# Where a delayed norm, a weight preparation and an activation store stand in the queues: three moves in a one-layer hybrid kernel

## The chip, the cores and the metric

The kernel runs on one core of a Trainium2 chip, as one launch. The metric is the device time of the program in microseconds (us): the median of several runs. The engines are TensorE (PE, with its weight loads as PEld), VectorE (DVE), ScalarE (ACT), GpSimd (POOL) and SyncE (SP). SP, ACT and POOL can issue DMAs; each works through its instructions in order, so that an issue that has to wait holds up whatever stands behind it on that engine.

## The reference

One layer of a streaming encoder for two groups of rows that share the weights: one prompt of 2048 rows and 8 sample sequences of 16 rows, all 1024 wide.

```python
h   = rms_norm(x, norm_g[0])
z   = h @ w_in                        # q, k, v of attention and of the mLSTM, gates
att = rms_norm(chunk_band_attention(z), g_att)        # 8 heads x 64
ml  = head_norm(mlstm(z)) * g_mlstm * sigmoid(o)      # 4 heads x 128
x   = x + rms_norm(concat([att, ml]) @ w_out, norm_g[1])          # "x2" below
u   = rms_norm(x, norm_g[2]) @ w_up                               # 2 x 2816 columns
y   = causal_conv(u, w_conv, width=3) + b_conv
gate, up = split(y)
x   = x + rms_norm((gelu(gate) * up) @ w_down, norm_g[3])
```

The outputs are the new rows and the new caches of attention, mLSTM and convolution.

## The kernel before, in words

The rows are cut into 17 tiles of 128 (16 of the prompt, one of the samples). Matrices are multiplied in a split form: both operands are written as a rounded part and a rest (`hi`, `lo`; names ending in `h` and `l`), and each product is three matmuls, lines L104, L105 and L106 of one helper. The split of a weight takes a CAST on ACT (`wuh`, L1301) and a subtraction on DVE (`wul`, L1302).

*Order.* The instructions are not run in the order of the code. A scheduler simulates a timeline and puts the instructions of each engine into an order by it. Instructions wrapped in `tc.keep_in_program_order` keep the code's order among themselves. Stages are written as generators that yield where other work may come between.

*The project stage* (`project`, 1052 to 1352 us in the trace) goes over the tiles: it loads the mixed rows (`mr`, L991), norms them, turns them (PE transposes into `mT_pt`; ACT writes the rounded part `mt` by a CAST, L210, DVE the rest, L211), multiplies by `w_out` into `wo` in two halves, copies each half out on DVE (L1029), sums squares on ACT (L1031), scales on DVE (L1041), adds the input row on POOL (L1042), and stores the result as `x2d` (L1043). The input row of a later tile is loaded into `mx` on SP (L1018) and waits for the buffer that the store of x2 reads. Beside this, the first part of the FFN begins: rows of x2 come back (`x2r`, L1084), ACT squares them (L1100), and the first up weights are fetched (`wu`, L1318) and combined (`ws`, L1330).

*The down-weight differences* (`folds`) are a preparation that runs beside the project stage. The FFN uses one level of a scheme with seven products in place of eight, which needs differences of the blocks of `w_down`. For each of `NK` = 11 groups, four blocks of 128x512 are loaded from `in_w_down` (SP, L1178), four differences are formed in place (DVE, L1183), and four blocks are stored to `wtd` in HBM (POOL, L1186). `project` steps this generator 4 times a tile.

*The FFN* runs in three blocks of 6, 6 and 5 tiles, each with an up stage over 22 features and a down stage. In an up stage the products of a feature are followed by copies on ACT and by additions (`uu`), the convolution (`y`, L1513 and L1514) and the gate (`g`, L1672 and L1675) on DVE, while SP fetches later weights (`wu`, L1348), each as soon as its buffer is free.

*Delayed norms.* The last norm of blocks 0 and 1 is done in the next block's up stage. The down stage has stored its result as `f0d` and `f1d`, two halves of 512 columns for each tile. `later` makes one unit for each half tile: it fetches the half into `f` (L1436) and the half row of x2 into `x` (L1437), multiplies by the row's factor and the norm's gains on DVE (L1439), adds `x` on POOL (L1440) and stores the output from POOL (L1441). `delayed` steps the units, once for each feature from the fourth on; there are 12 units in block 1's up stage and 12 in block 2's.

*Buffers.* `spare` is a pool of 6 buffers of 128x512 for one thing after another: four for a group of `folds`, two for a unit of `later`.

Of the kernel before, what the change touches and what calls it, by code (L numbers as in the profile page):

```python
# [13 lines left out]
ALU = mybir.AluOpType  # L14
# [26 lines left out]
NK = NF // 2  # L41
# [8 lines left out]
def hymba_step(ctx: ExitStack, tc: tile.TileContext, I: dict, O: dict):  # L50
    nc = tc.nc
# [17 lines left out]
    def spare_tile(name):  # L69
        return spare.tile([P, 512], F32, tag="k", name=name)  # L70

    def dt_(shape, name):
        return dram.tile(shape, F32, tag=name, name=name)
# [15 lines left out]
    def rsqrt_mean(ssq, n, name, eps=EPS):  # L89
        ms = small.tile([P, 1], F32, tag="ms", name=name + "_ms")  # L90
        mean_square(ms, ssq, n, eps)
        rs = small.tile([P, 1], F32, tag="rs", name=name + "_rs")
        nc.gpsimd.tensor_tensor(rs, ms, nhalf[:, 0:1], op=ALU.pow)  # L93
        return rs
# [30 lines left out]
    wtd = [dt_([P, 2048], f"wtd{k}") for k in range(NK)]  # L125
    wsd = [dt_([P, 2048], f"wsd{f}") for f in range(NF)]
    lated = [dt_([P, 4, 384], f"lated{i}") for i in range(4)]
    x2d = [dt_([P, D], f"x2d{t}") for t in range(17)]

    def x_src(t):  # L130
        return I["x_sample"] if t == SAMPLE else I["x_prompt"][t * P:(t + 1) * P, :]
# [69 lines left out]
    def rows_to_T(hrow, chunk, j, name, bank):  # L201
        w = 4 if bank is not ps_big else KT
        for q in range(KT // w):
            pt = bank(f"{name}_pt{q}")
            for k in range(w):
                transpose(pt[:, k * P:(k + 1) * P], hrow[:, (w * q + k) * P:(w * q + k + 1) * P])
            ptv = pt.rearrange("p (k t) -> p k t", k=w)
            hv = chunk[:, 0, w * q:w * q + w, j * P:(j + 1) * P]
            lv = chunk[:, 1, w * q:w * q + w, j * P:(j + 1) * P]
            nc.scalar.copy(hv, ptv)  # L210
            nc.vector.tensor_tensor(lv, ptv, hv, op=ALU.subtract)  # L211
# [4 lines left out]
    def rows_tile(tag, shape, name, dtype=F32):  # L216
        if tag == "xr":
            return rows.tile(shape, dtype, tag="xr", name=name, bufs=2)
        return pa.tile(shape, dtype, tag=tag, name=name, bufs=1)
# [750 lines left out]
    def drain():  # L970
        while any([p_.step() for p_ in pipes]):
            pass

    def project(tiles):

        ss = [SimpleNamespace(t=t) for t in tiles]
        fold = folds(3, 2)

        def load(s):
            t = s.t  # L980
            if t == 8:
                drain()
                open_ffn()
            s.m = rows_tile("xr", [P, D], f"mr{t}")
            if t == SAMPLE:
                for b in range(DB):
                    own = bass.AP(atts[b].tensor, atts[b].offset, [[512, DS], [DS * 512 + DA, HA], [1, DA]])
                    nc.sync.dma_start(s.m[b * DS:(b + 1) * DS, 0:512].rearrange("p (h d) -> p h d", h=HA), own)
                nc.sync.dma_start(s.m[:, 512:D], mixs)
            else:  # L990
                nc.sync.dma_start(s.m, mixd[t // 4][:, t % 4, :])  # L991

        def norm(s):
            mt = wpool.tile([P, 2112], F32R, tag="wh", name=f"mt{s.t}", bufs=2)
            ssq = small.tile([P, 1], F32, tag="ssq", name=f"assq{s.t}")
            nc.scalar.activation(mt[:, :512], s.m[:, :512], AF.Square, accum_out=ssq)
            rs = rsqrt_mean(ssq, 512, f"att{s.t}")
            nc.vector.tensor_scalar(s.m[:, :512], s.m[:, :512], rs, None, op0=ALU.mult)
            s.mt = mt[:, :2 * D].rearrange("p (a k n) -> p a k n", a=2, k=KT)

        def turn_rows(s):
            ffn.mt = s.mt
            rows_to_T(s.m, s.mt, 0, f"mT{s.t}", ps_mm if s.t < 8 else ps_big)

        load(ss[0])
        norm(ss[0])
        yield 0.0, 0.3
        turn_rows(ss[0])
        load(ss[1])
        yield 0.9, 1.2  # L1010
        for n_, s in enumerate(ss):
            t = s.t
            nxt = ss[n_ + 1] if n_ + 1 < len(ss) else None
            if nxt:
                norm(nxt)
            mx = wpool.tile([P, 2112], F32, tag="wl", name=f"mx{t}", bufs=2)
            m, xr = mx[:, 0:D], mx[:, D:2 * D]
            nc.sync.dma_start(xr, x_src(t))  # L1018
            for hf in range(2):
                c = slice(hf * 512, hf * 512 + 512)  # L1020
                acc = ps_mm(f"wo{t}_{hf}")
                for k in range(KT):
                    mm3(acc, s.mt[:, 0, k, :], s.mt[:, 1, k, :], wo[k][0][:, c], wo[k][1][:, c],
                        start=(k == 0), stop=(k == KT - 1))
                    if k % 4 == 3:
                        next(fold, None)
                        yield 2.6, 0.5
                ssq = small.tile([P, 1], F32, tag="wssq", name=f"wssq{t}_{hf}")
                nc.vector.tensor_copy(m[:, c], acc)  # L1029
                idle = m[:, 512:D] if hf == 0 else s.mt[:, 0, 0:4, :].rearrange("p k n -> p (k n)")  # L1030
                nc.scalar.activation(idle, m[:, c], AF.Square, accum_out=ssq)  # L1031
                if hf == 0:
                    ssa = ssq
                    mean_square(ssa, ssq, D)
                    if nxt:
                        turn_rows(nxt)
                        if n_ + 2 < len(ss):
                            load(ss[n_ + 2])
                        yield 0.9, 1.2
            rs = rsqrt_mean(ssq, D, f"n1_{t}", ssa)  # L1040
            nc.vector.scalar_tensor_tensor(m, m, rs, g1[0], op0=ALU.mult, op1=ALU.mult)  # L1041
            nc.gpsimd.tensor_tensor(xr, m, xr, op=ALU.add)  # L1042
            nc.gpsimd.dma_start(x2d[t], xr)  # L1043
        for _ in fold:
            pass

# [7 lines left out]
    def open_ffn():  # L1054

        p1.close()
        ffn.p3 = ctx.enter_context(tc.tile_pool(name="p3", bufs=2, reuse_waits="tile"))
        ffn.halo = ffn.p3.tile([P, 44, 2], F32, tag="halo", name="halo", bufs=1)
        nc.vector.memset(ffn.halo, 0.0)
        ffn.g2 = ffn.p3.tile([P, D], F32, tag="g2", name="g2", bufs=1)  # L1060
        nc.sync.dma_start(ffn.g2, I["norm_g"][2:3, :].broadcast_to([P, D]))
        pipes[:] = [Pipe(h2_units(0, lead=6)), Pipe(iter([]))]
# [107 lines left out]
            nc.scalar.copy(hi, lo.bitcast(F32))  # L1170
            nc.vector.tensor_tensor(lo, lo.bitcast(F32), hi, op=ALU.subtract)

    def folds(before, after):

        for k in range(NK):
            t = [spare_tile(f"fold{k}_{x}") for x in range(4)]
            for x in range(4):
                tc.keep_in_program_order(nc.sync.dma_start(t[x], I["w_down"][k][:, x * 512:(x + 1) * 512]))  # L1178
            for _ in range(before):
                yield  # L1180
            a, b, c, d = t
            for o, x, y in ((a, b, a), (b, c, b), (c, c, a), (d, d, c)):
                tc.keep_in_program_order(nc.vector.tensor_tensor(o, x, y, op=ALU.subtract))  # L1183
            yield
            for x in range(4):
                tc.keep_in_program_order(nc.gpsimd.dma_start(wtd[k][:, x * 512:(x + 1) * 512], t[x]))  # L1186
            for _ in range(after):
                yield

    GROUPS = ["va0", "qk0", "qk1", "va1", "qk2", "qk3", "qb0", "vo0", "qb1", "vo1", "qb2", "vo2", "qb3", "vo3"]  # L1190
    SRC = {g: i for i, g in enumerate(["va0", "qk0", "qk1", "va1", "qk2", "qk3",
# [45 lines left out]
    for n_, (half, gi) in enumerate(seq):  # L1237
        wh, wl, _ = pend
# [193 lines left out]
    def later(t, rs):  # L1432

        def unit(half):
            v, x, c = spare_tile(f"f{half}{t}"), spare_tile(f"x{half}{t}"), half * 512
            tc.keep_in_program_order(nc.sync.dma_start(v, (f0d, f1d)[half][t]))  # L1436
            tc.keep_in_program_order(nc.sync.dma_start(x, x2d[t][:, c:c + 512]))  # L1437
            yield 0.0, 0.0
            nc.vector.scalar_tensor_tensor(v, v, rs, g3[:, c:c + 512], op0=ALU.mult, op1=ALU.mult)  # L1439
            nc.gpsimd.tensor_tensor(v, v, x, op=ALU.add)  # L1440
            nc.gpsimd.dma_start(out_rows(t)[:, c:c + 512], v)  # L1441
            yield 0.0, 1.0

        return [unit(half) for half in range(2)]

    def delayed(units):

        for u, after in zip(units, units[1:] + [iter([])]):
            if u is units[0]:
                next(u)  # L1450
                yield
            next(after, None)
            next(u)
            yield

    ph.close()
    p4 = ffn.p4 = ctx.enter_context(tc.tile_pool(name="p4", bufs=1, side="right", reuse_waits="tile"))
# [3 lines left out]
    g3 = norm_row(3)  # L1461
# [14 lines left out]
    for b, tiles in enumerate(FBLOCKS):  # L1476
# [282 lines left out]
        for dh in range(2):  # L1759
# [57 lines left out]
            for j in order:  # L1817
# [5 lines left out]
                else:  # L1823
# [4 lines left out]
                    rs = p3.tile([P, 1], F32, tag=f"drs{j}", name=f"drs{tiles[j]}", bufs=2)  # L1828
# [101 lines left out]
```

## Time and profile before

| what | value |
|---|---|
| median of 3 runs | 2822.27 us (2820.95 to 2822.5) |
| the profiled execution's own time | 2824.88 us |
| its span | 2823.1 us |
| its granted PE clock, mean | 0.988 |
| PE busy | 2709.4 us, 96% of the span |
| DVE, ACT, POOL busy | 1877.5, 1516.3 and 646.3 us |
| project stage | 1052 to 1352 us |
| delayed norms in block 1's and block 2's up stage | about 1895 to 2095 and 2384 to 2558 us |

A row of waits reads: engine and line of the instruction that waited, what released it, us in total, times, the longest. A row of the timeline reads: start and duration in us, engine, line, operation, output and inputs, and in square brackets how long the engine had been idle before it and for what. A row of windows gives for each engine how long it was busy in the window, the clock that PE was granted (1.00 is full) and the share of time in which the DMA engines moved data. "SPq" is SP's queue.

### The profile page before, as it was taken

How to read it: one execution, taken by the hardware profiler on the slowest of the kernel's cores; microseconds unless marked ns; L12 is line 12 of the kernel's file. 1: busy time of each engine (PE TensorE's matmuls, PEld its weight loads, DVE VectorE, ACT ScalarE, POOL GpSimd, SP SyncE). 2: the span in 40 equal slices, each digit the busy share in tenths (PEclk: the TensorE clock that was granted, in tenths of full speed). 3: DMA queues.
4: the chain of work that ended last, by engine and by line, in shares of the span. 5: the costliest groups of instructions: out<-in, count | busy, mean ns of one | idle time of the engine just before them, and what ended most of it. 6: DMA issues, size and time to landing. Idle time of an engine off the chain costs nothing. (4 is left out here: it accounts for less than half of the span.)

```text
span 2823.1 us, 47537 instructions
## 1 busy us (share of the span) xinstructions
PE 2709.4 (96%) x16393; PEld 2530.2 (90%) x16393; DVE 1877.5 (67%) x3395; ACT 1516.3 (54%) x3164; POOL 646.3 (23%) x1249
## 2 busy tenths in 40 slices
PE   8899999999999999988999999999999999989998
PEld 7899999998899997877999997899999779889887
DVE  5344455655456677766888888657877866778744
ACT  4355455544356675533555557655555655556543
POOL 1000010211000013355344432023332202443200
PEclk9999999999999999999999999999999999999999
DMA  5544355556554566568665558756765876665655
GB/s 183 152 120 131 109 173 157 170 157 209 161 159 146 158 191 208 177 223 276 222 198 192 180 185 283 241 179 205 224 201 165 275 234 193 202 202 177 197 182 185
DMA packets 325296, 535.12 MB, mean 190 GB/s; under 512 B 59586, under 2 KB 156574, under 8 KB 324926
## 3 DMA queue, kind: packets, MB, share of 16 engines
q1 hardware_dynamic: 257598, 403.33, 47.3%
q0 software_dynamic: 28864, 94.92, 8.9%
q10 hardware_dynamic: 38592, 33.83, 3.6%
q8 instruction: 129, 2.11, 0.3%
q14 instruction: 113, 0.93, 0.1%
HBM read 383.87 MB, written 151.21 MB: 190 GB/s over the span
## 5 line engine op out<-in xcount | busy, mean ns | idle before, releaser
L104 PE MATMUL udc<-B,wuh 128*128 128x384 f32 (+1 forms) x720 | 237.7, 330 | 7.9 <-DVE uu L1648 7.9
L106 PE MATMUL udc<-B,wul 128*128 128x384 f32 (+1 forms) x720 | 236.7, 329 | 1.4 <-DVE wul L1302 1.4
L105 PE MATMUL udc<-B,wuh 128*128 128x384 f32 (+1 forms) x720 | 236.5, 328 | 0.0
L1302 DVE TENSOR_TENSOR wul<-wu,wuh 128x512 fp32r<-128x512 f32 x255 | 167.0, 696 | 30.7 <-ACT wuh L1301 29.6
L1301 ACT CAST wuh<-wu 128x512 fp32r<-128x512 f32 x255 | 144.2, 621 | 48.6 <-PE udc L105 43.8
L405 DVE CUSTOM_DVE_ANT_0 tmp<-s,nb 128x640 f32<-128x640 f32 (+4 forms) x128 | 94.3, 737 | 95.5 <-PE s L395 93.4
L104 PE MATMUL vo<-wi_h,hT 128*128 128x256 f32 x544 | 155.1, 285 | 0.6 <-DVE mt L211 0.6
L106 PE MATMUL vo<-wi_h,hT 128*128 128x256 f32 x544 | 155.5, 286 | 0.0
L105 PE MATMUL vo<-wi_l,hT 128*128 128x256 f32 x544 | 154.9, 285 | 0.0
L104 PEld LDWEIGHTS udc<-B,wuh 128*128 128x128 f32 x720 | 136.7, 190 | 10.5 <-DVE uu L1648 10.3
L406 ACT ACTIVATE tmp<-tmp,mn 128x640 f32<-128x640 f32 (+4 forms) x128 | 97.6, 762 | 76.0 <-DVE mn L405 74.6
L106 PEld LDWEIGHTS udc<-B,wul 128*128 128x128 f32 x720 | 136.5, 190 | 1.7 <-DVE wul L1302 1.7
L104 PE MATMUL qk<-hT,wi_h 128*128 128x384 f32 (+1 forms) x384 | 130.6, 340 | 7.1 <-ACT qk_st L236 6.2
L105 PEld LDWEIGHTS udc<-B,wuh 128*128 128x128 f32 x720 | 136.7, 190 | 0.2
L1302 DVE TENSOR_TENSOR wdl<-wdr,wdh 128x512 fp32r<-128x512 f32 x198 | 124.5, 684 | 13.0 <-ACT wdh L1301 12.9
L418 DVE TENSOR_TENSOR ptl<-pt,pth 128x640 fp32r<-128x640 f32 (+4 forms) x128 | 93.7, 737 | 57.4 <-ACT pth L417 56.4
L105 PE MATMUL qk<-hT,wi_h 128*128 128x384 f32 (+1 forms) x384 | 128.9, 336 | 0.0
L106 PE MATMUL qk<-hT,wi_l 128*128 128x384 f32 (+1 forms) x384 | 128.6, 335 | 0.0
L105 PE MATMUL qb<-hT,wi_h 128*128 128x384 f32 (+1 forms) x384 | 128.0, 333 | 0.0
L106 PE MATMUL qb<-hT,wi_l 128*128 128x384 f32 (+1 forms) x384 | 127.4, 332 | 0.0
L104 PE MATMUL qb<-hT,wi_h 128*128 128x384 f32 (+1 forms) x384 | 127.3, 331 | 0.0
L104 PE MATMUL dn<-wdh,ah 128*128 128x512 f32 x308 | 122.6, 398 | 3.9 <-ACT ah L1301 3.9
(450 smaller groups left out, 9291.0 us busy)
## 6 DMA issues: line engine op xcount, KB each, us to landing
wu<-in_w_up SPq DMA_DIRECT2D x220, 256.0 KB, 4.5
wu<-wsd SPq DMA_DIRECT2D x176, 256.0 KB, 4.0
wdr<-in_w_down SPq DMA_DIRECT2D x110, 256.0 KB, 4.6
wi_raw<-in_w_in SPq DMA_DIRECT2D x52, 512.0 KB, 4.0
wsd<-ws POOLq DMA_DIRECT2D x88, 256.0 KB, 3.8
wdr<-wtd SPq DMA_DIRECT2D x88, 256.0 KB, 5.3
ad_S<-s POOLq DMA_DIRECT2D x88, 192.0 KB, 3.2
ar<-ad_S SPq DMA_DIRECT2D x40, 384.0 KB, 5.2
```

The source lines that it names most:

```text
L104: nc.tensor.matmul(out, ah, bh, start=start, stop=False, skip_group_check=onto)
L105: nc.tensor.matmul(out, ah, bl, start=False, stop=False, skip_group_check=onto)
L106: nc.tensor.matmul(out, al, bh, start=False, stop=stop, skip_group_check=onto)
L405: nc.vector.tensor_tensor_reduce(o_, s_, b_, 1.0, 3e38, ALU.add, ALU.min, accum_out=mn)
L406: nc.scalar.activation(tmp[:, :n], tmp[:, :n], AF.Exp, bias=mn, scale=-1.0, accum_out=rsum[:, i % 4, hh:hh + 1])
L418: nc.vector.tensor_tensor(s.ptl[:, sl, qc], ptv, s.pth[:, sl, qc], op=ALU.subtract)
L1301: nc.scalar.copy(h, r)
L1302: nc.vector.tensor_tensor(l, r, h, op=ALU.subtract)
```

## The change

There are three edits.

1. `later` and `delayed`: a unit's multiply is kept in program order, and `delayed` finishes a unit in the step in which it fetches the next one, instead of fetching the next before it finishes the one at hand.
2. `folds`: loads and stores are issued on ACT instead of SP and POOL. The work of a group is spread over 6 steps by a plan: at step 0 the group before is stored and blocks a and b are loaded, at step 2 blocks c and d are loaded, at step 5 the differences are formed.
3. `project`: x2 is stored from SP instead of POOL.

```diff
     def project(tiles):
...
-        fold = folds(3, 2)
+        fold = folds(6, {0: ("before", "ab"), 2: ("cd",), 5: ("combine",)})
...
             nc.gpsimd.tensor_tensor(xr, m, xr, op=ALU.add)
-            nc.gpsimd.dma_start(x2d[t], xr)
+            nc.sync.dma_start(x2d[t], xr)
...
-    def folds(before, after):
-
-        for k in range(NK):
-            t = [spare_tile(f"fold{k}_{x}") for x in range(4)]
-            for x in range(4):
-                tc.keep_in_program_order(nc.sync.dma_start(t[x], I["w_down"][k][:, x * 512:(x + 1) * 512]))
-            for _ in range(before):
-                yield
-            a, b, c, d = t
+    def folds(period, plan):
+
+        live = {}
+
+        def load(k, xs):
+            if k < NK:
+                for x in xs:
+                    live[k, x] = spare_tile(f"fold{k}_{x}")
+                    tc.keep_in_program_order(nc.scalar.dma_start(live[k, x], I["w_down"][k][:, x * 512:(x + 1) * 512]))
+
+        def combine(k):
+            a, b, c, d = [live[k, x] for x in range(4)]
             for o, x, y in ((a, b, a), (b, c, b), (c, c, a), (d, d, c)):
                 tc.keep_in_program_order(nc.vector.tensor_tensor(o, x, y, op=ALU.subtract))
-            yield
-            for x in range(4):
-                tc.keep_in_program_order(nc.gpsimd.dma_start(wtd[k][:, x * 512:(x + 1) * 512], t[x]))
-            for _ in range(after):
+
+        def store(k):
+            if k >= 0:
+                for x in range(4):
+                    tc.keep_in_program_order(nc.scalar.dma_start(wtd[k][:, x * 512:(x + 1) * 512], live.pop((k, x))))
+
+        acts = dict(ab=lambda k: load(k, (0, 1)), cd=lambda k: load(k, (2, 3)), combine=combine, store=store,
+                    before=lambda k: store(k - 1))
+        for k in range(NK):
+            for step in range(period):
+                for what in plan.get(step, ()):
+                    acts[what](k)
                 yield
+        if live:
+            store(NK - 1)
...
             yield 0.0, 0.0
-            nc.vector.scalar_tensor_tensor(v, v, rs, g3[:, c:c + 512], op0=ALU.mult, op1=ALU.mult)
+            tc.keep_in_program_order(
+                nc.vector.scalar_tensor_tensor(v, v, rs, g3[:, c:c + 512], op0=ALU.mult, op1=ALU.mult))
...
     def delayed(units):
 
-        for u, after in zip(units, units[1:] + [iter([])]):
-            if u is units[0]:
-                next(u)
-                yield
-            next(after, None)
+        for u in units:
             next(u)
             yield
+            next(u)
```

The changed kernel's lines have other numbers: the loads, differences and stores of `folds` are L1181, L1186 and L1191, the delayed norm's multiply is L1453, the weight split L1314 and L1315.

DVE at the first delayed norm of block 2, before; `f` is the fetched half, `drs` the row's factor, `norm_row` the gains, `wul` a weight's rest, the number after the name of a weight its feature:

```order
2805 L1514 SCALAR_TENSOR_TENSOR y_0_0_26716<-ug_0_26592,wcv,y_0_0_26716 128x656
2806 L1302 TENSOR_TENSOR wul_6_26882<-wu_12_1_26883,wuh_6_26881 128x512
2807 L1439 SCALAR_TENSOR_TENSOR f_27055<-f_27055,drs_26318,norm_row_16400 128x512
2808 L1302 TENSOR_TENSOR wul_6_26882<-wu_12_2_26885,wuh_6_26881 128x512
2809 L1302 TENSOR_TENSOR wul_6_26882<-wu_12_4_26887,wuh_6_26881 128x512
```

The same multiply in the changed kernel:

```order
2845 L1315 TENSOR_TENSOR wul_10_27196<-wu_13_2_27199,wuh_10_27195 128x512
2846 L1315 TENSOR_TENSOR wul_10_27196<-wu_13_4_27201,wuh_10_27195 128x512
2847 L1315 TENSOR_TENSOR wul_10_27196<-wu_13_3_27203,wuh_10_27195 128x512
2848 L1453 SCALAR_TENSOR_TENSOR f_27055<-f_27055,drs_26318,norm_row_16400 128x512
2849 L1315 TENSOR_TENSOR wu_11_2_27280<-wu_3_0_27282,wu_11_0_27278 128x512
2850 L1315 TENSOR_TENSOR wu_11_2_27280<-wu_13_5_27284,wu_11_0_27278 128x512
```

It has moved from row 2807 to row 2848 of DVE, from among the splits of `wul_6` to behind those of `wul_10`. The place of its fetch among SP's weight loads is the same as before.

ACT in the project stage at the first rows of x2 that come back, before; `mt` by L210 is the cast that PE's next `wo` needs, `x2r` are the two halves' rows:

```order
1469 L1031 ACTIVATE mt_14937,wssq_1_15284<-mx_15167 128x512
1470 L996 ACTIVATE mt_15294,assq_15295<-mr_15249 128x512
1471 L1031 ACTIVATE mx_15302,wssq_0_15333<-mx_15302 128x512
1472 L1100 ACTIVATE B_0_15383,fssq_15386<-x2r_15367 128x8x128
1473 L1100 ACTIVATE B_0_15383,fssq_15392<-x2r_15369 128x8x128
1474 L210 CAST mt_15294<-mT_pt_15337 128x1024
```

The same tile in the changed kernel, with a turn from one group of `folds` to the next ahead of it:

```order
1506 L1031 ACTIVATE mt_14933,wssq_1_15280<-mx_15163 128x512
1507 L996 ACTIVATE mt_15290,assq_15291<-mr_15245 128x512
1508 L1191 DMA wtd_247<-fold_1_14962 128x512
1509 L1191 DMA wtd_247<-fold_2_15086 128x512
1510 L1191 DMA wtd_247<-fold_3_15088 128x512
1511 L1181 DMA fold_0_15264<-in_w_down 128x512
1512 L1181 DMA fold_1_15266<-in_w_down 128x512
1513 L1181 DMA fold_2_15313<-in_w_down 128x512
1514 L1181 DMA fold_3_15315<-in_w_down 128x512
1515 L1031 ACTIVATE mx_15298,wssq_0_15329<-mx_15298 128x512
1516 L1100 ACTIVATE B_0_15379,fssq_15382<-x2r_15359 128x8x128
1517 L210 CAST mt_15290<-mT_pt_15333 128x1024
```

The cast has come ahead of the second Square on `x2r`; seven stores and loads of the weight preparation now stand before the tile's Square and cast (the eighth, the store of block a, is two rows further up).

SP near the end of the project stage, before:

```order
657 L1120 DMA lated_278<-t_16156 512x1x128
658 L1178 DMA fold_2_16195<-in_w_down 128x512
659 L1318 DMA wu_2_16348<-in_w_up 128x512
660 L1318 DMA wu_3_16350<-in_w_up 128x512
661 L1178 DMA fold_3_16196<-in_w_down 128x512
```

The same place in the changed kernel:

```order
628 L1120 DMA lated_278<-t_16152 512x1x128
629 L1331 DMA wu_2_16348<-in_w_up 128x512
630 L1331 DMA wu_3_16350<-in_w_up 128x512
631 L1043 DMA x2d_293<-mx_16052 128x1024
632 L1331 DMA wu_0_16390<-in_w_up 128x512
```

The fold loads are gone from between the up weights, and a store of x2 has come in behind them.

## The prediction

> **What bounds the kernel now.** I read the stages as windows first, then the waits of each engine in the stages that the change touches, then single turns in order of time. The windows are the project stage, block 1's up stage with its delayed norms, and block 2's; columns are the window, its length, the busy time of PE, PEld, DVE, ACT and POOL, the granted clock, the DMA share and GB/s:
>
> ```profile
> 1052.00:1352.00 300.00, 275.89 (x1433) 227.82 (x1432) 214.68 (x350) 131.68 (x318) 138.02 (x200) 0.96 0.69 224
> 1895.00:2095.00 200.00, 193.17 (x1105) 191.91 (x1104) 158.74 (x222) 112.41 (x196) 74.23 (x124) 1.00 0.70 215
> 2384.00:2558.00 174.00, 155.16 (x987) 151.94 (x988) 131.12 (x210) 96.66 (x201) 73.21 (x128) 0.95 0.63 202
> ```
>
> TensorE (PE) is the bound: it loses 24 us of 300 in the project stage, 7 of 200 in block 1 and 19 of 174 in block 2, whose clock is down to 0.95. Only this idle time and the slow clock can be won. Next, what DVE waits for in the two FFN windows (two rows for block 1, two for block 2; waiter, releaser, total us, times, longest), then PE in the same windows (two rows, then four), and last PE's two largest in block 0's up stage (1400 to 1680), which has no delayed norms:
>
> ```profile
> DVE f L1439 <- DMA f<-f1d: 16.6, 4, 4.6
> DVE f L1439 <- DMA f<-f0d: 4.4, 3, 1.7
> DVE f L1439 <- DMA f<-f1d: 19.2, 6, 4.7
> DVE f L1439 <- DMA f<-f0d: 16.0, 6, 4.7
> PE ue L106 <- DVE wul L1302: 3.5, 2, 1.8
> PE udc L104 <- DVE uu L1648: 3.3, 2, 2.0
> PE ue L106 <- DVE wul L1302: 8.8, 6, 3.2
> PE ue L104 <- ACT wuh L1301: 3.6, 2, 2.1
> PE udc L104 <- ACT udc L1608: 3.6, 1, 3.6
> PE udc L104 <- DVE uu L1648: 2.8, 2, 1.9
> PE ue L106 <- DVE wul L1302: 1.9, 3, 0.6
> PE udc L104 <- DVE uu L1648: 1.0, 3, 0.4
> ```
>
> DVE stands 56.2 us before the delayed norm's multiply, waiting for its fetch. PE's waits name other releasers, but these are the work queued on DVE behind that multiply. One turn of it, in order of time: SP issues the fetch, the multiply waits 2.14 us for it, the weight split wul that PE needs starts only behind it and its neighbours, and PE has stood 1.82 us:
>
> ```profile
> 2415.38 0.39 SPq L1436 DMA_DIRECT2D f<-f0d  x1
> 2420.29 0.75 DVE L1439 SCALAR_TENSOR_TENSOR f<-f,drs,norm_row 128x512 f32<-128x512 f32 x1 [2.14 <-DMA f<-f0d]
> 2421.13 1.67 POOL L1440 TENSOR_TENSOR f<-f,x 128x512 f32<-128x512 f32 x1 [2.80 <-DVE f L1439]
> 2421.57 1.39 DVE L1675 TENSOR_TENSOR g<-y,y 128x128 f32<-128x128 f32 x1
> 2424.62 1.89 DVE L1302 TENSOR_TENSOR wul<-wu,wuh 128x512 fp32r<-128x512 f32 x3
> 2425.96 0.42 PE L106 MATMUL ue<-B,wul 128*128 128x320 f32 x1 [1.82 <-DVE wul L1302]
> ```
>
> **Part 1: the norms later behind their fetches.** Nothing is added; 24 multiplies on DVE move, and with them the POOL adds and output stores. In the new order the first norms of block 2 stand some 40 DVE rows further back: the first one now comes right behind the wul splits that ran from 2424.62 on. The fetch was issued 4.9 us before the multiply started, wait included; 40 rows of DVE are some 25 us (131.12 us in 210 instructions, 0.62 each). So f's wait goes.
>
> What could take its place is SP: three units fill the six buffers, so the fourth unit's fetch, on SP with the weight loads behind it, now waits until the first unit is stored. Its place on SP before (first row), what SP does next (second), and how long a store of this size lands (the wtd stores, 5.7 us):
>
> ```profile
> 2428.68 0.38 SPq L1436 DMA_DIRECT2D f<-f1d  x1
> 2440.32 1.07 SPq L1348 DMA_DIRECT2D wu<-in_w_up  x2
> wtd<-fold POOLq DMA_DIRECT2D x44, 256.0 KB, 5.7
> ```
>
> The multiply at about 2427.5, 0.75 + 1.67 for it and the add, and issue and landing of 6 us give 2436. SP would stand 7 us at the fetch; but behind it, it stood until 2440.32 anyway, so this costs nothing. Without that cover it would be up to 7 us a unit.
>
> What PE regains is its waits: 3.5 + 3.3 = 6.8 us in block 1 and 8.8 + 3.6 + 3.6 + 2.8 = 18.8 in block 2, together 25.6. Beside it stands the clock. After the gap of 1.82 us PE soon issues at a pace of 0.27 us (first two rows) instead of 0.14 to 0.15 (last two, from before the gap):
>
> ```profile
> 2427.01 0.47 PE L106 MATMUL ue<-B,wul 128*128 128x320 f32 x1
> 2427.28 0.47 PE L104 MATMUL ue<-B,wuh 128*128 128x320 f32 x1
> 2423.69 0.31 PE L105 MATMUL ua<-B,wu 128*128 128x320 f32 x1
> 2423.83 0.31 PE L106 MATMUL ua<-B,wu 128*128 128x320 f32 x1
> ```
>
> A dozen matmuls at 0.12 us more are 1.4 us a time. The clock of 0.95 instead of 1.00 bounds all such losses in block 2 at 0.05 x 174 = 8.7 us; I take five times 1.4, 7 us. The Trainium skill ("TensorE: Matmul & The Clock Gate", section "Part 1: The HAM clock gate") has the clock fall after an idle window of about 3.4 us. By it only the wait of 3.6 us would count, the term would be 1.4 and the time 5.6 us higher; the trace speaks against that, since here 1.82 us was enough.
>
> Not all of 25.6 + 7 = 32.6 us comes back. Block 0, without norms, still waits 1.9 + 1.0 = 2.9 us in 280; in 200 + 174 us that is 3.9. The gain is **28.7 us**; its ends are 32.6 and 6 (the last rival).
>
> **Part 2: the down-weight differences on ScalarE's queue.** SP loses 44 loads and POOL 44 stores; ACT gets 88 DMAs. What such an issue costs ACT (lowest, median, highest ns), and SP's two largest waits in the project stage:
>
> ```profile
> L287 ACTq DMA_DIRECT2D vobd<-vo_st x68: 326/326/353, 258.3 to 1052.9; - x68
> SPq L1178 <- DMA wtd<-fold: 51.5, 13, 16.4
> SPq L1018 <- DMA x2d<-mx: 48.5, 11, 10.0
> ```
>
> ACT pays 88 x 0.33 = 29 us; of 300 it is busy 131.68, so the issues as such are covered. SP's 51.5 us of standing for a buffer moves to ACT in part: a fold's last two loads take buffers whose stores ACT has just issued. Four issues (1.3 us) of a landing of 5.7 leave 4.4 us in which ACT stands, and behind it the Squares and the casts of the next tile's transposed rows (mt, L210), for which PE waits. There are 10 such turns. In about half of them the new order puts work of the tile between stores and loads, so that the landing is over, and ACT is idle more than half the time; I take 2 of 10 as reaching PE. Each costs 4.4 us and then slow clock, for which I take 2.3 a time, an estimate out of the 12 us that 0.96 against 1.00 makes of the whole stage. 2 x 6.7 = **13.4 us added**; ends 0 and 67.
>
> **Part 3: x2 stored from SP, and what POOL and SP lose.** Two gaps carry most of the project stage's loss. Their rows, then ACT's second Square on x2's rows, POOL's add and x2 store, and two issues of SP:
>
> ```profile
> PE wo L104 <- ACT mt L210: 8.0, 2, 7.3
> PE wo L104 <- DVE mx L1029: 6.2, 1, 6.2
> 1231.75 1.06 ACT L1100 ACTIVATE B<-x2r 128x1024 fp32r<-128x1024 f32 x1 [2.49 <-DMA x2r<-x2d]
> 1206.85 2.39 POOL L1042 TENSOR_TENSOR mx<-mx 128x1024 f32<-128x1024 f32 x1
> 1212.16 0.58 POOL L1043 DMA_DIRECT2D x2d<-mx  x1
> 1319.39 0.53 SPq L1120 DMA_DIRECT2D lated<-t  x1
> 1323.75 0.33 SPq L1178 DMA_DIRECT2D fold<-in_w_down  x1
> ```
>
> The first (7.3 us) comes from two Squares on rows of x2 ahead of the cast that PE wants. In the new order the second stands behind the cast: 1.06 + 2.49 = 3.6 us off. The x2 store left POOL 2.9 us after its add had ended, behind two wtd stores that are gone: 2.9 more. With 2.3 of slow clock that is 8.8. The second (6.2 us) is DVE waiting for up weights before it copies, and their loads stood on SP behind a fold load that was released 4.4 us after SP's issue before it; that load is gone: 4.4. Together **13.2 us off**; ends 0 and 18.1 (both gaps whole, with 2.3 each). SP now waits for POOL's add at each x2 store, but the load behind it (L1018) waited for that store's landing already (48.5 us), so nothing new is queued there.
>
> **The sum.** 2824.9 us profiled (span 2823.1) - 28.7 + 13.4 - 13.2 = 2796.4. The profiled run lies 2.6 above the median of 2822.3, so the median becomes **2794**.
>
> **The rivals.** *ACT's landing waits eat the project stage.* If 4 to 6 of the 10 turns reach PE, 5 x 6.7 = 33.5 us stand against 28.7 + 13.2 = 41.9 of gain: 2822.3 - 8.4 = 2814. For it: PE's largest wait in the stage is on ACT. Against: ACT is busy 44% of it. *Slower:* the same mechanism, from (41.9 + 5.6) / 6.7, some 7 turns on; at 9 the time is 2822.3 - 41.9 + 60.3 = 2841. It needs ACT to be urgent at nearly every turn, where PE waited for mt only twice in the stage. *The cost is the POOL add, not the wait.* Beside the add of the turn shown, DVE's g step took 1.39 us; alone it takes 0.28:
>
> ```profile
> 2476.22 0.28 DVE L1675 TENSOR_TENSOR g<-y,y 128x128 f32<-128x128 f32 x1
> ```
>
> That 1.1 us goes with the add wherever the multiply stands; 24 times it is 26.4 of the 32.6 us, part 1 brings 6, and the time is 2816. Against it: all the waits of the multiply together are 56.2 us, more than twice as much. The Trainium skill ("SBUF — State Buffer", section "SBUF: two separate sides") says that a DVE operation with two SBUF inputs and a GpSimd operation that reads SBUF shut each other out of a shared port; the two rows here agree with it.
>
> **How the numbers follow.** The forecast has 0.71, the rival near 2814 0.12, the slower one 0.09, the add 0.08. A difference of 0.2% (5.6 us) is about what a measurement of this kernel can tell from none, so "same" is 2816.7 to 2827.9. Faster: 0.71, 0.08 of the 0.12 and 0.05 of the 0.08, together 0.84. Same: 0.04 and 0.03, 0.07. Slower 0.09. The range goes from all gains and no new wait (2822.3 - 32.6 - 13.2 = 2777) to just past the add's 2816, at 2817; outside lie the slower case and the upper parts of the other two, together under 0.2.
>
> **What would show it.** In the changed profile DVE's waits of f for f0d and f1d fall from 56.2 us below 8; PE's busy share rises above 0.96 in block 2's delayed norms, with a clock of 0.99 or more, and above 0.98 in block 1's. In the project stage SP's 51.5 us are gone and waits of ACT's queue on fold loads and stores appear, 20 to 45 us, of which at most 15 are passed on to PE. I am wrong in part 1 if PE still waits 15 us or more in the two windows although f's waits are gone, and in parts 2 and 3 if the project stage grows by more than 5 us.

## The result and the profile after

The changed kernel takes 2787.22 us (2786.8 to 2788.39) against 2822.39 for the kernel before, which has a fourth run now; the ratio is 0.9873, with a 95% interval of 0.9856 to 0.989. The forecast was 2794, with a range of 2777 to 2817. The profiled execution took 2786.82 us, its span is 2785.1.

First the stages as windows, each from the first matmul of the stage to the first of the next: project, block 0's up stage, block 1's up stage, block 2's up stage. Before:

```profile
1052.75:1349.67 296.92, 272.81 (x1414) 224.74 (x1413) 211.82 (x346) 129.65 (x313) 137.07 (x198) 0.96 0.69 223
1349.67:1681.07 331.40, 324.06 (x1828) 319.50 (x1828) 288.85 (x428) 193.07 (x332) 138.79 (x240) 0.99 0.59 195
1854.98:2181.89 326.91, 320.08 (x1830) 318.60 (x1829) 247.21 (x350) 187.83 (x332) 105.03 (x186) 1.00 0.64 196
2356.04:2656.85 300.81, 281.19 (x1843) 277.27 (x1842) 223.78 (x378) 179.29 (x379) 109.40 (x223) 0.97 0.61 190
```

And after:

```profile
1049.22:1343.51 294.29, 274.38 (x1414) 224.25 (x1413) 218.13 (x343) 130.57 (x312) 105.39 (x137) 0.98 0.68 224
1343.51:1677.81 334.30, 326.00 (x1828) 319.96 (x1828) 290.65 (x431) 192.84 (x332) 143.58 (x239) 0.99 0.58 194
1854.78:2173.82 319.04, 319.04 (x1831) 318.81 (x1830) 251.04 (x350) 187.96 (x332) 103.39 (x186) 1.00 0.65 201
2347.63:2620.07 272.44, 271.06 (x1842) 269.84 (x1841) 222.75 (x378) 178.49 (x379) 105.80 (x223) 1.00 0.68 210
```

Block 2's up stage is 28.4 us shorter and block 1's 7.9, together 36.2 by the unrounded rows. The project stage is 2.6 shorter and block 0's up stage 2.9 longer. In block 2, 18.2 us of the 28.4 are idle time of PE (length less busy time: 19.6 before, 1.4 after), and 10.1 are busy time over the same matmuls, most of it the clock (0.97 before, 1.00 after; the part on why the prediction was right splits it). Block 1's PE is not idle at all any more (6.8 us before), at a clock of 1.00 in both. The spans differ by 38 us; the remaining 2 lie in stages that no edit touches, and such stages differ between executions: with the same code and order up to it, the project stage began at 1048.9 to 1058.4 us in the traces of this case.

What DVE waits for in block 2's up stage now (its two largest), what PE waits for there (both rows), and SP at the delayed norms' fetches:

```profile
DVE wul L1315 <- ACT wuh L1314: 14.6, 9, 5.6
DVE uu L1676 <- PE udc L106: 9.2, 7, 3.6
PE udc L104 <- DVE uu L1659: 0.8, 1, 0.8
PE ue L106 <- DVE wul L1315: 0.6, 1, 0.6
SPq L1450 <- DMA out_y_prompt<-f: 21.2, 7, 5.3
SPq L1449 <- POOL f L1454: 4.3, 3, 1.6
```

No wait of DVE for `f` is left, and PE's 19.6 us of idle time in the stage have become 1.4. The first unit of block 2, from its fetch to its store, and the fourth unit's fetch of `x`, which takes the first one's buffer:

```profile
2377.41 0.37 SPq L1449 DMA_DIRECT2D f<-f0d  x1
2407.27 0.74 DVE L1453 SCALAR_TENSOR_TENSOR f<-f,drs,norm_row 128x512 f32<-128x512 f32 x1
2408.09 1.67 POOL L1454 TENSOR_TENSOR f<-f,x 128x512 f32<-128x512 f32 x1 [0.69 <-DVE f L1453]
2410.07 0.56 POOL L1455 DMA_DIRECT2D out_y_prompt<-f  x1 [0.31 <-POOL f L1454]
2414.74 0.32 SPq L1450 DMA_DIRECT2D x<-x2d  x1
```

The multiply comes 30 us behind its fetch and waits for nothing. SP now stands at such fetches, 25.5 us in all in block 2, and PE, idle 1.4 us there, pays nothing that can be seen.

In the project stage, SP's two largest waits, ACT's behind the weight differences' DMAs (the second is a store that waits for DVE to form the differences), and the matmuls at the places of the two large gaps:

```profile
SPq L1043 <- POOL mx L1042: 90.0, 14, 15.1
SPq L1018 <- DMA x2d<-mx: 15.6, 7, 2.5
ACT mx L1031 <- DMA wtd<-fold: 11.1, 1, 11.1
ACT b L1129 <- DVE fold L1186: 6.9, 1, 6.9
ACT num L715 <- DMA fold<-in_w_down: 5.9, 1, 5.9
ACT jk L654 <- DMA wtd<-fold: 1.7, 1, 1.7
1228.31 0.68 PE L104 MATMUL wo<-wo,mt 128*128 128x512 f32 x1 [2.17 <-ACT mt L210]
1331.05 0.79 PE L106 MATMUL wo<-wo,mt 128*128 128x512 f32 x1 [2.12 <-DVE mt L211]
```

The gaps of 7.3 and 6.2 us have shrunk to 2.2 and 2.1, which is 9.2 us; but the stage's idle time of PE fell only from 24.1 to 19.9 us, and its length by 2.6. The rest went into small waits: PE has 31 gaps in the stage where it had 24. And what the project stage gains, block 0's up stage gives back. In the six profiles with the old project stage (before and experiments below) the two stages together take 624.1 to 629.8 us, 627.4 on the mean; in the four with the differences on ACT in their planned form 626.0 to 628.6, on the mean 627.2. The project stage alone is 3 us shorter in the latter (292.6 against 295.7 on the mean), the next stage as much longer.

### The profile page after: what moved, and what is told of

It is laid out like the page before. It is cut to its first block, busy times and chain, and to the rows that moved or that the text cites. A ratio compares the mean times of both kernels' runs of the same rounds, so it can differ in the third digit from the quotient of the medians.

```text
span 2785.1 us, 47504 instructions
## 1 busy us (share of the span) xinstructions
PE 2700.7 (97%) x16393; PEld 2521.4 (91%) x16393; DVE 1889.0 (68%) x3395; ACT 1516.5 (54%) x3164; POOL 615.9 (22%) x1188
## 4 chain that ended last, share of the span: by engine, by line
PE 46%; DVE 6%; DMA 4%; issue 2%; ACT 1%; POOL 1%; ACTq 0%; DVEq 0%; SPq 0%; POOLq 0%
PE udc L104 5%; PE udc L105 5%; PE udc L106 5%; PE dn L106 3%; PE dn L104 3%; PE dn L105 3%; PE ua L104 3%; PE ua L106 2%; PE ua L105 2%; DMA wu<-in_w_up 2%; PE dnm L106 2%; PE dnm L105 2%; PE dnm L104 2%; PE ue L106 1%; PE ue L104 1%
## 5 line engine op out<-in xcount | busy, mean ns | idle before, releaser
L1315 DVE TENSOR_TENSOR wul<-wu,wuh 128x512 fp32r<-128x512 f32 x255 | 168.7, 702 | 33.3 <-ACT wuh L1314 31.1
L1314 ACT CAST wuh<-wu 128x512 fp32r<-128x512 f32 x255 | 144.4, 621 | 54.4 <-PE udc L105 50.1
L1315 DVE TENSOR_TENSOR wdl<-wdr,wdh 128x512 fp32r<-128x512 f32 x198 | 124.5, 684 | 11.3 <-ACT wdh L1314 11.2
```

Source lines behind the costliest of these rows:

```text
L1314: nc.scalar.copy(h, r)
L1315: nc.vector.tensor_tensor(l, r, h, op=ALU.subtract)
```

## The experiments

Where a kernel's times were taken on another chip than another's, its ratio to the kernel before on its own chip is given, with the 95% interval. The kernel before had medians of 2821.5 to 2825.3 there.

**The first edit alone.** The kernel before with `later` and `delayed` of the changed one.

> The kernel before with the first edit alone (multiply kept in order, delayed finishing a unit before it fetches the next); weight differences and x2 store as before. Theory (f's wait was the cost, and the edits in the project stage are worth about 3 us): 2786 to 2792 us, block 2's up stage 271 to 274 us long, block 1's 318 to 320, project stage 295 to 298. Rival (the edits in the project stage carry a third of the gain): 2797 to 2802.

2788.15 us, ratio 0.9864 (0.9846 to 0.9881). Block 1's up stage is 319.0 us, block 2's 272.7, the project stage 293.0, which is 2 us less than the theory allowed. The first edit is the whole gain.

**The second and third edit alone.** The changed kernel with `later` and `delayed` as before.

> The second and third edit alone: differences on ACT's queue in two parts, x2 stored from SP, delayed norms as before. Theory: 2817 to 2822 us, block 2's up stage still about 300 us with 35 us of DVE waits for f. Rival (a third of the gain): 2808 to 2812.

2822.25 us, ratio 0.9995 (0.9982 to 1.0009). Block 2's up stage stays at 298.9 us, with 33.6 us of DVE's waits for `f`. The two edits in the project stage bring nothing that can be measured.

**What in the first edit does it.** In one kernel the multiply of the kernel before is kept in program order and nothing else is changed; in the other, `delayed` is rewritten and the multiply left free.

```diff
-            nc.vector.scalar_tensor_tensor(v, v, rs, g3[:, c:c + 512], op0=ALU.mult, op1=ALU.mult)
+            tc.keep_in_program_order(
+                nc.vector.scalar_tensor_tensor(v, v, rs, g3[:, c:c + 512], op0=ALU.mult, op1=ALU.mult))
```

> The kernel before with the multiply kept in program order, and nothing else; delayed still fetches the next unit before it finishes the one at hand. Theory (holding the multiply back from its early place is all that the first edit does): within 0.15% of the run with the whole first edit, 2786 to 2793 us, waits for f below 5 us. Rival (the other order of the steps in delayed is needed as well): 2810 us or more, waits for f above 20 us.

> The kernel before with the other order of the steps in delayed, but the multiply not kept in program order. Theory (the scheduler puts the multiply back to its early place): as before, 2812 to 2830 us, DVE waits for f above 45 us, block 2's up stage 298 to 302 us. Rival (the order of the steps alone does part of it): 2805 us or less.

Kept only: 2789.76 us, ratio 0.9872 (0.9856 to 0.9889). The other order only: 2823.69 us, ratio 1.0 (0.9983 to 1.0017). Block 2's up stage, the window of the first and of the second:

```profile
2351.81:2624.51 272.70, 271.12 (x1842) 269.89 (x1841) 223.00 (x378) 178.45 (x379) 107.89 (x223) 1.00 0.68 209
2356.30:2656.80 300.50, 280.61 (x1842) 276.19 (x1841) 223.76 (x378) 179.25 (x379) 109.28 (x223) 0.97 0.61 190
```

DVE waits 33.3 us for `f` in this stage of the second, and not at all in the first. One wrapped line is the whole change in time. The code of the kernel before already finished a unit one feature after its fetch; the scheduler had pulled the multiply forward again (presumably because its simulated fetch lands sooner than the real one; that was not looked into).

**Wait or add.** Two effects could make an early multiply dear: its wait for the fetch, and the POOL add behind it, which slows DVE. Each was taken away by itself from the kernel before, and the add from the changed one as well. The one without the wait reads the resident gains:

```diff
-            tc.keep_in_program_order(nc.sync.dma_start(v, (f0d, f1d)[half][t]))
...
-            nc.vector.scalar_tensor_tensor(v, v, rs, g3[:, c:c + 512], op0=ALU.mult, op1=ALU.mult)
+            nc.vector.scalar_tensor_tensor(v, g3[:, c:c + 512], rs, g3[:, c:c + 512], op0=ALU.mult, op1=ALU.mult)
```

The ones without the add lose one line:

```diff
-            nc.gpsimd.tensor_tensor(v, v, x, op=ALU.add)
```

> The kernel before without POOL's add in the delayed norms (it stores the normed half row without the residual, for the 24 units; all fetches stay). Theory (the wait for the fetch is the cost): DVE's waits for f stay above 45 us in all, 2815 to 2822 us. Rival (DVE beside the add is the cost, 1.1 us in 24 places): 2794 to 2800 us.

> The kernel before, with the multiply reading the gains (resident) in place of the fetched half; the 24 fetches of f are left out, the fetches of x, the adds and the stores stay, so the multiply has no DMA to wait for, and its output is not the norm. Its place on DVE is again early, some 15 rows behind that of before. Theory (the wait costs most, the add costs only what is added to a wait): block 2's up stage 272 to 280 us, 2790 to 2800 us. Rival (wait and add cost alike, wherever the multiply is early): block 2's up stage 285 to 292 us, 2804 to 2812 us.

> The changed kernel without POOL's add in the delayed norms (it stores the normed half without the residual). Theory (without the wait DVE has the time that the add takes from it): within 0.15% of the changed kernel, block 2's up stage 271 to 273 us. Rival (the add still costs): 268 us or less, 5 us or more off the time.

| | with the add | without it |
|---|---|---|
| multiply waits for its fetch | kernel before: block 2's up stage 300.8 us | 290.6 us; 2809.25 us, ratio 0.9943 (0.9923 to 0.9964) |
| it doesn't wait | resident operand: 272.0 us; 2786.41 us, ratio 0.9873 (0.9851 to 0.9896); changed kernel: 272.4 us | changed kernel without the add: 271.5 us; 2789.11 us, ratio 0.9878 (0.986 to 0.9896) |

The waits of DVE and of PE in block 2's up stage without the add, in the kernel before:

```profile
DVE f L1439 <- DMA f<-f1d: 18.8, 6, 4.2
DVE f L1439 <- DMA f<-f0d: 16.7, 6, 4.9
PE ue L106 <- DVE wul L1302: 7.5, 6, 4.0
PE ue L104 <- ACT wuh L1301: 2.1, 2, 1.8
PE udc L104 <- DVE uu L1647: 1.2, 2, 0.8
PE udc L104 <- ACT udc L1607: 1.1, 1, 1.1
```

DVE waits as long as before (35.5 us against 35.2), but PE waits 11.9 us in the stage where it had been idle for 19.6. Without the wait, the add costs the stage less than 1 us (272.4 against 271.5); beside it, 10.2. The reading that fits all of this is that the wait uses up the lead that DVE has on PE, and that the add costs time only where this lead is gone already; the lead itself was not measured. The theory of the wait alone expected 2815 or more without the add, and was wrong in that; the rival, that the add alone is the cost, expected 2800 or less and was wrong as well. The resident operand brought the whole gain, a little more than the 2790 to 2800 expected. One caution: with a resident operand the scheduler also placed the multiply some 15 DVE rows later than before, and 24 fetches are missing.

**ACT's cover.** In the changed kernel each store of the differences is issued twice:

```diff
-                    tc.keep_in_program_order(nc.scalar.dma_start(wtd[k][:, x * 512:(x + 1) * 512], live.pop((k, x))))
+                    t = live.pop((k, x))
+                    for _ in range(2):
+                        tc.keep_in_program_order(nc.scalar.dma_start(wtd[k][:, x * 512:(x + 1) * 512], t))
```

> The changed kernel with every store of the weight differences issued twice from ACT (44 more DMAs of 256 KB, to the same place). Theory (ACT has the time; a turn reaches PE now and then by some 1 to 2 us): project stage 294 to 300 us, whole time up by less than 0.25%. Rival (each turn hands its wait to PE): 10 turns by 2 us or more, project stage 310 us or more.

2817.03 us, ratio 0.9983 (0.9969 to 0.9996), where the changed kernel has 0.9873. PE's largest wait in the project stage and the stage's window:

```profile
PE wo L104 <- ACT mt L210: 20.2, 7, 9.3
1050.80:1369.00 318.20, 277.87 (x1413) 227.75 (x1412) 213.26 (x343) 129.51 (x311) 100.17 (x138) 0.95 0.71 232
```

The stage is 23.9 us longer, and PE waits for casts of ACT (20.2 us, where it waited 3.6 in the changed kernel). The theory was wrong and the rival right in size, though with 7 waits instead of 10 turns: ACT, busy 129.51 us of 318, did not hide 44 more DMAs, whose issue by itself would be 15 us. Each extra store also brings its transfer and holds a buffer longer; these were not told apart.

**Each edit of the project stage without the other.** First x2 from POOL as before, then the weight differences as before (loads on SP, stores on POOL), each in the changed kernel:

```diff
-            nc.sync.dma_start(x2d[t], xr)
+            nc.gpsimd.dma_start(x2d[t], xr)
```

> The changed kernel with x2 stored from POOL as before. Theory (the store's queue matters for the two gaps only through the stores that stood before it, and these are gone from POOL): within 0.15% of the changed kernel, SP's 90 us of waits for POOL's add gone and some 50 us for the landing of x2 back. Rival (SP's place is worth the 3 us that its issue came late): 2 to 6 us slower, the gap near 1226 us back above 4 us.

```diff
-        fold = folds(6, {0: ("before", "ab"), 2: ("cd",), 5: ("combine",)})
+        fold = folds(3, 2)
...
```

> The changed kernel with the weight differences as before (loads on SP, stores on POOL, one part), so the first and third edit. Theory (the second edit brings nothing and costs nothing in sum): within 0.2% of the changed kernel, project stage 291 to 297 us. Rival (the second edit frees SP for the up weights and x2, which the third needs to bring anything): 5 us or more slower than the changed kernel, both large gaps of the project stage above 5 us.

x2 from POOL: 2787.37 us, ratio 0.9872 (0.9854 to 0.989), project stage 291.2 us, and SP's 90 us of waits for POOL's add gone, as the theory had it. The two large gaps stay small, so the second edit is enough to shrink both:

```profile
1230.25 0.50 PE L104 MATMUL wo<-wo,mt 128*128 128x512 f32 x1 [1.84 <-ACT mt L210]
1333.39 0.80 PE L106 MATMUL wo<-wo,mt 128*128 128x512 f32 x1 [3.33 <-DVE mt L211]
```

Differences as before: 2795.66 us (2793.55 to 2801.3), ratio 0.9907 (0.9886 to 0.9929), project stage 303.8 us. SP in the latter, and PE's three largest waits:

```profile
SPq L1178 <- DMA wtd<-fold: 45.7, 12, 17.9
SPq L1043 <- POOL mx L1042: 44.3, 9, 11.0
PE mT_pt L76 <- DVE mr L998: 6.8, 2, 6.1
PE wo L104 <- DVE mx L1029: 5.3, 1, 5.3
PE wo L104 <- ACT mt L210: 3.5, 2, 2.9
```

The run with the first edit alone is the one to set beside this: its ratio is 0.9864 (0.9846 to 0.9881) and its project stage 293.0 us. So moving the store of x2 to SP costs some 10 us while SP still carries the fold loads (10.8 in the stage's length), and nothing once they are gone. The theory was wrong here, and the rival right in the time but only half right in the gaps. The second large gap stays at 5.3 us, but the first is down to 2.9, from 5.7 with the first edit alone: the third edit by itself shrinks it too.

**The same medicine elsewhere.** In block 0's up stage of the changed kernel DVE waits 25.7 us for up weights at sums that stand early (ws). They were kept in program order too:

```diff
-                nc.vector.tensor_tensor(o, x, y, op=op)
+                tc.keep_in_program_order(nc.vector.tensor_tensor(o, x, y, op=op))
```

> The changed kernel, and the combinations of up weights in block 0's up stage and ahead of it (ws, L1343) kept in program order too, which puts them some 15 DVE rows further back. Theory (a multiply or sum that stands early before a DMA costs PE time wherever DVE has no time to spare): DVE's 25.7 us of waits for wu in that stage fall below 8, PE's waits there from 8.3 below 4, 3 to 8 us off the time. Rival (DVE has time there, since those waits cost PE little now): within 0.15% of the changed kernel.

2846.91 us, ratio 1.0086 (1.0064 to 1.0108): 60 us slower than the changed kernel, and the rival was wrong as well as the theory. All of it is in block 0's up stage. PE's two largest waits there and the stage's window:

```profile
PE udc L104 <- ACT wuh L1314: 21.7, 7, 5.0
PE udc L104 <- ACT wu L1314: 15.8, 4, 5.2
1346.00:1743.70 397.70, 350.52 (x1830) 336.34 (x1829) 301.39 (x443) 202.17 (x337) 144.03 (x249) 0.92 0.52 170
```

DVE's wait for `wu` is no longer among its waits, as meant, and the stage is 63 us longer. These sums are the weights of PE's next products, so what is put back is what PE needs; 39 us are idle time more and 25 busy time more, at a clock of 0.92 instead of 0.99. SP's fetches are held up too: it stands 199.5 us there for buffers that these sums still hold (77.9 in the changed kernel). Which link of the chain from sum to cast came late first was not settled.

## Why the prediction was right, point by point

**What bounds the kernel.** Right. PE's idle time and clock in the two windows were the whole gain as far as it can be seen, and DVE's wait for the fetch was behind the releasers that PE's rows named: with the wait gone, the waits for `wul`, `wuh`, `udc` and `uu` went too.

**Part 1.** The mechanism was right, the size too small. Forecast 28.7 us, ends 6 and 32.6; measured 36.2 in one profile each, above the upper end. The two terms that were counted came out: PE's idle time, 25.6, fell by 25.1 (18.2 and 6.8). The clock, taken at five times 1.4 us, was five stretches of 3.41 us at a granted clock of 0.50 in block 2's stage (2426.85 to 2430.26 us is one), and none after. The 63 matmuls that start in them kept PE busy for 16.9 us; at the changed kernel's 0.147 us each they would take 9.3. So the clock cost 7.6 us, and the bound of 8.7 held. Two things were missing. PE's busy time fell by 3.6 us more, 2.5 in block 2 and 1.0 in block 1, whose clock is 1.00 in both kernels. This seems to go with the gaps: block 1's four gaps at 0.26 us each make the 1.0, and ten fewer in block 2 would make 2.6, an estimate from that. And the 3.9 us that were to stay did not: the idle time left is 1.4 us in block 2 and none in block 1. Block 0's stage was no fair measure of it: there DVE also forms the sums (ws).

**SP's new stand at the fetch.** Right, and smaller in block 2: at most 5.3 us a time instead of 7, hidden as argued. In block 1 it is nothing new: SP stood there for 18.6 us before, at most 4.8 a time, and stands 23.7 now, at most 6.1.

**Part 2 and part 3.** The net of +13.4 and -13.2 was 0.2; measured, -2.6 us in the profile, and a ratio of 0.9995 (0.9982 to 1.0009) for both edits alone. The sum was right; of its two terms the runs bear out the 13.2 in size and not the 13.4, so that they cancelled may be luck. For the 13.2: the large gaps shrank by 9.2 us, and the stretches at half clock that begin at them went from 20.5 to 10.2 us, which is worth up to 5.1, so the size fits. Of this the stage kept some 3, and the next stage gave those back: a gap here is not a price, PE gains it and waits elsewhere. The earlier store of x2, to which 2.9 us of the first gap were put, comes with either edit. With x2 still on POOL it leaves 0.3 us after its add, since no store of the differences is ahead of it, and with the third edit but not the second the gap shrinks by 2.9 as well.

For the 13.4 of ACT: some 5 us of idle time did come in elsewhere in the stage, but as small waits of PE and not as two turns of 6.7, and no run says that they are ACT's. A store on ACT's queue landed after 4.3 us instead of the 5.7 taken, and the issue of a load took 0.46 us instead of 0.33 (medians). ACT stood 25.6 us for these DMAs, within the 20 to 45 expected, and PE waited 3.6 us for its casts. The doubled stores show that ACT can't carry twice as many. "Nothing new is queued there", of SP behind the store of x2, was wrong by itself: the run without the second edit is slower, and only with the fold loads off SP does the move cost nothing.

**The rivals.** ACT's waits did not eat the stage; with 44 more DMAs the stage grew by 23.9 us. The add was rightly put as a rival, but it is no alternative to the wait: it adds to it.

## What to carry to other kernels

When PE waits for a busy engine's ordinary work, look at what that engine waited for just ahead of it: an operation nobody needs soon, standing early before a DMA, can cost the time of what is queued behind it. Holding such an operation back is worth a line of code, but only where its result is not urgent: the same line on the sums of the next weights cost 60 us. Sum idle time and the fall of the busy time together: of the 36.2 us, 11.2 were busy time, 7.6 of them the slow clock after gaps.

## What the runs showed of the hardware

The length of a gap does not say whether PE's clock falls after it. In the kernel before, 1.82 us of idle time were followed by half pace (shown with the prediction), while after 2.35 us the pace stayed full:

```profile
2512.92 0.41 PE L106 MATMUL ue<-B,wul 128*128 128x320 f32 x1 [2.35 <-DVE wul L1302]
2513.76 0.31 PE L105 MATMUL ue<-B,wuh 128*128 128x320 f32 x1
2513.90 0.31 PE L106 MATMUL ue<-B,wul 128*128 128x320 f32 x1
2514.05 0.31 PE L104 MATMUL ue<-B,wuh 128*128 128x320 f32 x1
```

How a gap lies does say it, in these traces. The granted clock changes only at the borders of a fixed row of stretches of 3.41 us each. In block 2's up stage of the kernel before, PE was idle for more than 1 us in eight such stretches: behind 1.82, 1.89, 2.12, 2.20 and 2.70 us the next stretch was at half clock, behind 1.14, 1.36 and 1.62 us it was not. The gap of 2.35 us lies across a border, with 1.62 us ahead of it. In all 13 traces, from 1350 us on, the full clock never fell behind a stretch with less than 1.65 us of idle time, and always behind one with more than 1.85, about half of a stretch (idle time by the modelled ends of the matmuls).

The Trainium skill ("TensorE: Matmul & The Clock Gate", section "Part 1: The HAM clock gate") says that the window that is watched runs freely; that fits the fixed row of stretches, but its figure of about 3.4 us for an idle window does not fit the fall after 1.82 us, and the measurement decides.
